# Eight convolution taps on TensorE in place of sixteen, an order for the early output products, and a wait ahead of GpSimd's additions

## The chip, the cores and the metric

The kernel runs on one core of one Trainium2 chip. The metric is the device time of one execution in microseconds (us). The profile is of one further execution; its span is the time from its first to its last instruction. Engines are named as in the profile: PE is TensorE's matmul, PEld its weight load, DVE is VectorE, ACT is ScalarE, POOL is GpSimd, SP is SyncE, which issues transfers.

## The reference

Two layers of an encoder block on 512 tokens of width 1024, in float32. Cut to what matters here:

```python
for l in range(2):
    x = x + 0.5 * swiglu(rms_norm(x, g1), w_gate1, w_up1, w_down1)     # 1024 -> 2816 -> 1024
    p = rms_norm(x, gm) @ w_in                                         # latents of q and k/v, 2 x 512 conv columns
    attn = mla_group(...)          # 8 heads of 96 (64 + 32 rotary), keys and queries RMS-normed, chunk-causal
    u = a * sigmoid(g)             # a, g: the conv columns of p, 512 each
    y = causal_depthwise_conv(u, conv_w) + conv_b                      # 31 taps, one filter per column
    conv = silu(layer_norm(y, lg, lb))
    x = x + concat([attn, conv], -1) @ w_out                           # 1024 -> 1024
    x = x + 0.5 * swiglu(rms_norm(x, g2), w_gate2, w_up2, w_down2)
    x = rms_norm(x, gp)
```

## The kernel before

`x` lies transposed in on-chip memory: 8 tiles of 128 features by 512 tokens. Each product of float32 operands is made of three matmuls (`mm3`, L165 to L169): both operands are split into a high and a low part (ScalarE casts the high part, VectorE subtracts for the low part: `split`, L171), and high x high, high x low and low x high are added up in one bank of PSUM. A `group` (L238) runs `mm3` over the tiles `k` of the contraction. Each layer is a feed-forward block (`ffn`), a mix block (`mix`) and another feed-forward block. The change lies wholly in `mix_body` (L629 to L1022), which is run once per layer.

The order of work within an engine is not that of the program text alone. A planner orders the instructions at build time by the text's order, by priorities (`tc.high_priority`) and by its own estimate of when each is ready, and on the chip every engine works its queue off in that fixed order. `tc.issue_after(i)` holds the instructions traced in its block behind `i` on the engine of `i`.

The mix block runs as follows.

- Projections: convolution columns, query latents, key latents. `keys` (L803) makes the keys of four token tiles. For each, GpSimd computes a reciprocal root (`rsqrt`, a power, L185), which is remembered as `order["keys"]` (L813), and VectorE scales the key tile `kn` (L815 to L819).
- The convolution's gated input `u` is in 4 chunks of 128 columns (`glu`, L640). `TAPS` says which engine makes the 31 taps of a chunk. Chunks 0 and 3 are summed by VectorE in a PSUM bank `acc` (L964). Chunks 1 and 2 are made in pairs: ScalarE multiplies `u` by one tap into a buffer `pr` (L968; four buffers), GpSimd adds it to `ys[c]` (L970). For chunk `PC` = 2 the first `PT` taps come from TensorE instead: `conv_pe` (L667), with 4 column groups of 32, against the diagonal matrices `diag` that GpSimd prepares (L632). The additions of chunk 1 from tap `PAUSE` = 16 on, and all of chunk 2, are held behind `order["keys"]` on GpSimd (L969). So are the transfers of the first four output weights `wo` (L949, L154), which GpSimd issues.
- Attention in eight heads, as a pipeline: transposes (L844, L849) and their eviction (L846, L851), `scores` (L868 to L876: matmul, maximum on VectorE, exponential on ScalarE), transposes of the probabilities (L891 to L894), `values` (L902 to L916), and the split of two heads' outputs into one of the four tiles of `at` (L173, L174). `conv_pe` stands between the steps of this pipeline.
- The convolution's layer norm is a chain at high priority (L986 to L997). GpSimd adds `ys[0]`, `ys[1]` and `ys[2]` (L988, L989), VectorE adds `ys[3]` (L990), TensorE makes the mean (`pm`, L992), VectorE subtracts it (L994), ScalarE squares and VectorE adds the squares (L203). TensorE sums them over the columns (`sums`, L210), VectorE, GpSimd and VectorE turn this into a scale per token (L217, L185, L225), and TensorE spreads it over the partitions (`spread`, L229). Then VectorE scales, ScalarE applies silu (L1006, L1008) and the results `cv` are split.
- The output product has 8 contraction tiles: 4 of `at`, 4 of `cv`. For the first `WOG` = 4 output tiles the `at` half is computed early, while the chain runs (`early_groups`, L978). Output tile 0 (`E1` = 1) stands in the text before the chain and tiles 1 to 3 behind it; all are held only behind the last head's scores on TensorE, and the planner fills them in. The `cv` half follows (L1012 to L1022).

Of the kernel before, what the change touches and what calls it, by code (L numbers as in the profile page):

```python
# [7 lines left out]
FP = mybir.dt.float32  # L8
# [4 lines left out]
ALU = mybir.AluOpType  # L13
AX = mybir.AxisListType

P = 128
D = 1024
S = 512
L = 2
KD = D // P  # L20
NT = S // P
H = 8
DN = 64
DR = 32
DQ = DN + DR
# [14 lines left out]
CHUNKS = ((0, 2), (2, 5), (5, 8), (8, 11))  # L40
TAPS = (0, 31, 31, 0)
Q = 32
PT = 16
PC = 2
PSTEP = 3
AHEAD = 2
# [4 lines left out]
GLUP = 0  # L51
EARLY = "s"
PRELOAD = 1
E1 = 1
WOG = 4
CHAIN = 400
WAKE = 10
# [6 lines left out]
VECS = [("g1", 8), ("gm", 8), ("g2", 8), ("gp", 8), ("gql", 3), ("gkl", 2),  # L64
        ("cw", 4 * CK), ("cb", 4), ("lg", 4), ("lb", 4), ("gq", 1), ("gk", 1), ("cp", PT)]
VOFF = {}
# [6 lines left out]
CI32 = 256  # L73
# [4 lines left out]
def encoder_kernel(ctx: ExitStack, tc: tile.TileContext, xT, consts, vecs, rgain, wgu1, wd1, wdq1,  # L78
# [11 lines left out]
    def nm(s):  # L90
        uid[0] += 1
        return f"{s}{uid[0]}"
# [4 lines left out]
    def tmp(w=S, dt=FP):  # L97
        return tmps.tile([P, w], dt, tag="t", name=nm("t"))

    def bank():  # L100
        return psum.tile([P, S], FP, tag="ps", name=nm("ps"))

    def behind(ins):
        stack = ExitStack()
        for i in ins:
            stack.enter_context(tc.issue_after(i))
        return stack

    def conv_bank():
        return psum.tile([P, S], FP, tag="cv", name=nm("cv"), bufs=1)  # L110

    def tiny(tag, w, dt=FP):
        return small.tile([P, w], dt, tag=tag, name=nm(tag))

    V, A, G, T = nc.vector, nc.scalar, nc.gpsimd, nc.tensor

    x = cpool.tile([P, KD, S], FP, name="x")
    cst = cpool.tile([P, CN], FP, name="cst")
# [12 lines left out]
    minus_half = cpool.tile([P, H], FP, name="minus_half")  # L131
# [10 lines left out]
    def vv(l, name):  # L142
        o, w = VOFF[name]
        return vec[:, l, o:o + w]

    def load_w(src, w, kind=""):
        raw = wpool.tile([P, WC], FP, tag="raw", name=nm("raw"), bufs=3)
        nc.sync.dma_start(out=raw[:, :w], in_=src)
        hi = wpool.tile([P, WC], FR, tag="wh", name=nm("wh"))
        order["cast"] = A.copy(hi[:, :w], raw[:, :w]).ins  # L150
        lo = low()
        if kind == "sum":
            A.activation(lo[:, :w], raw[:, :w], AF.Copy, scale=-1.0)
            G.dma_start(out=lo[:, :w], in_=src, accum_op=ALU.add)  # L154
            return hi, lo
        (G if kind in POOLW.split() else V).tensor_tensor(lo[:, :w], raw[:, :w], hi[:, :w].bitcast(FP),  # L156
                                                          ALU.subtract)
        return hi, lo
# [2 lines left out]
        return wpool.tile([P, WC], FR, tag="wl", name=nm("wl"))  # L161

    order = {}

    def mm3(o, lh, ll, rh, rl, first, last, free=False):  # L165
        T.matmul(o, lh, rh, start=first, stop=False, skip_group_check=free)  # L166
        T.matmul(o, lh, rl, start=False, stop=False, skip_group_check=free)  # L167
        order["mm"] = T.matmul(o, ll, rh, start=False, stop=last, skip_group_check=free).ins  # L168
        return order["mm"]  # L169
# [13 lines left out]
    def rsqrt(y, ve):  # L183

        return G.tensor_tensor(y, ve, minus_half[:, 0:y.shape[1]], ALU.pow).ins  # L185
# [36 lines left out]
    def spread(r, made=bank, dg=None):  # L222

        dg = tmp() if dg is None else dg
        V.tensor_tensor(dg.rearrange("p (t j) -> p t j", t=NT),  # L225
                        ident[:, None, :].to_broadcast([P, NT, P]),
                        r[:, :, None].to_broadcast([P, NT, P]), ALU.mult)
        ps = made()
        order["spread"] = T.matmul(ps, ones, dg, start=True, stop=True).ins  # L229
        return ps  # L230
# [7 lines left out]
    def group(o, w, rhs, ks, n, ts=slice(0, S)):  # L238

        for k in ks:  # L240
            c = slice(k * P, (k + 1) * P)
            order["product"] = mm3(o, w[0][:, c], w[1][:, c], rhs[k][0][:, ts], rhs[k][1][:, ts], k == 0, k == n - 1)
# [382 lines left out]
    def mix(l, gx, norm, done):  # L625
        with tc.tile_pool(name="k", bufs=4) as kpool:
            mix_body(kpool, l, gx, norm, done)

    def mix_body(kpool, l, gx, norm, done):  # L629
        u, order = [], {}  # L630
        diag = kpool.tile([P, PT, Q], FP, tag="m", name=nm("m"), bufs=11)
        G.tensor_tensor(diag, cst[:, None, CI32:CI32 + Q].to_broadcast([P, PT, Q]),  # L632
                        vv(l, "cp")[:, :, None].to_broadcast([P, PT, Q]), ALU.mult)
        shifted = []

# [31 lines left out]
        def conv_pe():  # L667

            ps = bank()
            for a in range(PT // 4):  # L670
                for i in range(4):
                    T.matmul(ps[i * Q:(i + 1) * Q, 4 * a:], diag[:, 4 * a + i], shifted[i][:, 0:S - 4 * a],  # L672
                             start=a == 0, stop=a == PT // 4 - 1)
            A.activation(ys[PC], ps, AF.Identity, bias=vv(l, "cb")[:, PC:PC + 1])
# [9 lines left out]
        kn = kpool.tile([P, NT, H, DQ], FP, tag="kn", name=nm("kn"), bufs=1)  # L684
# [109 lines left out]
        def up_kv(w, t, n=S):  # L794

            ts_ = slice(t * P, (t + 1) * P)
            ps = bank()
            for k in range(2):
                cs = slice(k * n, (k + 1) * n)
                mm3(ps, ckT[k][0][:, ts_], ckT[k][1][:, ts_], w[0][:, cs], w[1][:, cs], k == 0, k == 1)  # L800
            return ps

        def keys():  # L803
            wk = load_w(wkv[l, 0], WC, "uk")
            for t in range(NT):
                ps = up_kv(wk, t)
                A.copy(kn[:, t, :, 0:DN], ps.rearrange("p (h d) -> p h d", h=H))
                j = tmp()
                A.activation(j, ps, AF.Square)
                V.tensor_reduce(ssk[:, t], j.rearrange("p (h d) -> p h d", h=H), axis=AX.X, op=ALU.add)  # L810
                V.tensor_scalar(ssk[:, t], ssk[:, t], ckc[:, t:t + 1], None, ALU.add)
                sck = small.tile([P, H], FP, tag="sck", name=nm("sck"))
                order["keys"] = rsqrt(sck, ssk[:, t])  # L813
                scp = small.tile([P, H], FP, tag="scp", name=nm("scp"))
                V.tensor_scalar(scp, sck, ratio[:, t:t + 1], None, ALU.mult)  # L815
                V.tensor_tensor(kn[:, t, :, 0:DN], kn[:, t, :, 0:DN],
                                sck[:, :, None].to_broadcast([P, H, DN]), ALU.mult)
                V.tensor_tensor(kn[:, t, :, DN:DQ], cke[:, t, None, :].to_broadcast([P, H, DR]),  # L818
                                scp[:, :, None].to_broadcast([P, H, DR]), ALU.mult)  # L819


        first = groups([wcv[l, 0], wcv[l, 1]], gx)
# [12 lines left out]
        at = []  # L835
# [3 lines left out]
        heads = [{} for _ in range(H)]  # L839
# [109 lines left out]
        with tc.issue_after(order["keys"]):  # L949
            wo = [load_w(wout[l, m], WC, "sum") for m in range(WOP)]  # L950
        cw, cb = vv(l, "cw"), vv(l, "cb")
        for c, n in enumerate(TAPS):
# [4 lines left out]
            for s in range(n, CK):  # L957
                k = CK - 1 - s
# [6 lines left out]
            for s in range(PT if c == PC else 1, n):  # L965
                k = CK - 1 - s
# [8 lines left out]
                V.tensor_tensor(ys[c][:, n:], ys[c][:, n:], acc[:, n:], ALU.add)  # L975
        early = []

        def early_groups(ms):  # L978
            with tc.issue_after(heads[H - 1][EARLY]):
                for m in ms:  # L980
                    early.append(bank())
                    group(early[m], wo[m], at, range(4), KD)

        early_groups(range(E1))
        st = Stats()
        with tc.high_priority(CHAIN):  # L986
            ysum = u[1]
            G.tensor_tensor(ysum, ys[0], ys[1], ALU.add)  # L988
            G.tensor_tensor(ysum, ysum, ys[2], ALU.add)  # L989
            V.tensor_tensor(ysum, ysum, ys[3], ALU.add)  # L990
            pm = conv_bank()
            T.matmul(pm, onesm, ysum, start=True, stop=True)  # L992
            for c in range(4):
                V.tensor_tensor(ys[c], ys[c], pm, ALU.subtract)  # L994
                st.add(ys[c], eng=V, into=(u[2], u[1], diag.rearrange("p a b -> p (a b)"), u[1])[c])
            r = st.token(CW, conv_bank)
            pr = spread(r, conv_bank, u[1])  # L997
        if PRELOAD:
            with behind(heads[H - 1]["exps"]):
                A.activation(tiny("pre", 1), ysum[:, 0:1], AF.Silu)  # L1000
        early_groups(range(E1, WOG))
        lg, lb = vv(l, "lg"), vv(l, "lb")
        cv = []
        for c in range(4):
# [7 lines left out]
        for m0 in range(0, KD, WOG):  # L1012
            ms = range(m0, min(m0 + WOG, KD))
# [272 lines left out]
```

## Time and profile before

| | |
|---|---|
| Time, median of 3 runs | 1802.54 us (1801.73 to 1802.81) |
| The profiled execution's own time | 1799.38 us |
| Its span | 1797.6 us |
| PE, PEld busy | 1780.6 us (99%), 1579.2 us (88%) |
| DVE, ACT, POOL busy | 1501.2 us (84%), 1093.8 us (61%), 384.1 us (21%) |
| Granted TensorE clock | 0.999 |

Busy times are sums over the whole span; matmuls are pipelined, so that a full PE column is not PE at its peak. In layer 0 attention and convolution lie between about 437 and 522 us of the span, in layer 1 between about 1326 and 1411 us; a stretch of time says more there than the sums do. In a timeline a row has start, duration, engine, line and operation, output and inputs, count, and in brackets the engine's idle time before it and what ended it.

### The profile page before, as it was taken

The numbers are of one execution on the slowest core, as the hardware profiler recorded it, in microseconds if no ns is written. First come the engines' busy times: TensorE is split into PE (matmuls) and PEld (weight loads), VectorE is DVE, ScalarE is ACT, GpSimd is POOL, SyncE is SP. The second block draws the span as 40 slices with busy tenths as digits, with TensorE's granted clock in tenths as the row PEclk, the third lists the DMA queues.
The fourth block names the chain that finished last, engine by engine and source line by source line (L and its number), as shares of the span: only waits on it lengthen the run. The fifth ranks groups of instructions, "written<-read, shape, count | busy, mean of one in ns | idle before, by whom it ended". The sixth has DMA issues, their size and how long they took to land.

```text
span 1797.6 us, 29443 instructions
## 1 busy us (share of the span) xinstructions
PE 1780.6 (99%) x11430; PEld 1579.2 (88%) x11430; DVE 1501.2 (84%) x2309; ACT 1093.8 (61%) x1699; POOL 384.1 (21%) x313
## 2 busy tenths in 40 slices
PE   9999999999999999999999999999999999999998
PEld 7899999888668899999888999998976788999997
DVE  7898988589965989898779989876999568989883
ACT  5665756467853575756645666554777435657564
POOL 1000000258722000000310000002685310000002
PEclk9999999999999999999999999999999999999999
DMA  5657574325203466665426575743260136575742
GB/s 169 168 134 186 130 180 119 109 88 128 61 24 100 125 166 161 153 161 127 125 63 170 127 191 125 193 109 114 77 171 7 35 92 162 138 181 135 182 118 73
DMA packets 71947, 228.28 MB, mean 127 GB/s; under 512 B 8448, under 2 KB 9600, under 8 KB 71808
## 3 DMA queue, kind: packets, MB, share of 16 engines
q1 hardware_dynamic: 55536, 171.87, 30.6%
q0 software_dynamic: 16128, 54.53, 18.0%
q8 instruction: 89, 1.46, 0.3%
q14 instruction: 50, 0.41, 0.1%
q10 hardware_dynamic: 144, 0.00, 0.0%
HBM read 222.19 MB, written 2.10 MB: 125 GB/s over the span
## 4 chain that ended last, share of the span: by engine, by line
PE 89%; DVE 7%; ACT 1%; issue 1%; POOL 1%; DMA 1%; SPq 0%; ACTq 0%; DVEq 0%
PE ps L166 23%; PE ps L167 23%; PE ps L168 23%; PE ps L385 11%; PE ps L386 6%; DVE cv L964 1%; DVE mx L872 1%; PE ps L913 1%; POOL sck L185 1%; DVE r L894 0%; DVE kn L818 0%; PE ps L891 0%; PE ps L210 0%; DVE r L851 0%; PE ps L672 0%
## 5 line engine op out<-in xcount | busy, mean ns | idle before, releaser
L166 PE MATMUL ps<-r,wh 128*128 128x256 f32 (+1 forms) x2556 | 811.6, 321 | 6.8 <-ACT r L173 5.7
L167 PE MATMUL ps<-r,wh 128*128 128x256 f32 (+1 forms) x2556 | 813.5, 319 | 0.1
L168 PE MATMUL ps<-r,wl 128*128 128x256 f32 (+1 forms) x2364 | 755.6, 321 | 0.0
L166 PEld LDWEIGHTS ps<-r,wh 128*128 128x128 f32 x2556 | 483.7, 189 | 53.2 <-ACT r L173 7.3
L167 PEld LDWEIGHTS ps<-r,wh 128*128 128x128 f32 x2556 | 484.9, 190 | 36.7 <-DVE r L174 1.5
L168 PEld LDWEIGHTS ps<-r,wl 128*128 128x128 f32 x2364 | 448.6, 190 | 34.3 <-DVE wl L156 0.2
L385 PE MATMUL ps<-xj,wh 128*128 128x512 f32 x864 | 303.8, 391 | 0.0
L150 ACT CAST wh<-raw 128x1024 fp32r<-128x1024 f32 (+3 forms) x148 | 132.3, 900 | 210.1 <-PE ps L167 131.1
L256 ACT CAST wh<-fr 128x1024 fp32r<-128x1024 f32 (+1 forms) x160 | 157.8, 986 | 104.6 <-DVE fr L422 49.3
L402 POOL DMA_DIRECT2D ls<-in_wgu x72 | 62.5, 868 | 734.7 <-ACT ls L401 502.6
L156 DVE TENSOR_TENSOR wl<-raw,wh 128x1024 fp32r<-128x1024 f32 (+3 forms) x132 | 143.4, 1093 | 91.0 <-ACT wh L150 90.3
L258 DVE TENSOR_TENSOR wl<-fr,wh 128x1024 fp32r<-128x1024 f32 (+1 forms) x160 | 181.8, 1137 | 20.1 <-ACT wh L256 20.1
L385 PEld LDWEIGHTS ps<-xj,wh 128*128 128x128 f32 x864 | 161.4, 188 | 30.1
L386 PE MATMUL ps<-xj,ls 128*128 128x256 f32 x576 | 161.3, 280 | 0.0
L970 POOL TENSOR_TENSOR y<-y,pr 128x495 f32<-128x495 f32 (+29 forms) x90 | 121.7, 1353 | 46.4 <-ACT pr L968 41.0
L256 ACT CAST wh<-raw 128x1024 fp32r<-128x1024 f32 (+1 forms) x100 | 98.1, 981 | 45.1 <-PE ps L167 24.2
L258 DVE TENSOR_TENSOR wl<-raw,wh 128x1024 fp32r<-128x1024 f32 (+1 forms) x100 | 113.3, 1133 | 14.3 <-ACT wh L256 13.8
L386 PEld LDWEIGHTS ps<-xj,ls 128*128 128x128 f32 x576 | 108.3, 188 | 0.0
L401 ACT ACTIVATE ls<-fr 128x1024 fp32r<-128x1024 f32 (+1 forms) x56 | 56.1, 1002 | 75.6 <-PE ps L386 41.5
L203 POOL TENSOR_TENSOR r<-r,t 128x512 f32<-128x512 f32 x45 | 74.2, 1658 | 130.2 <-ACT t L199 129.7
L964 DVE SCALAR_TENSOR_TENSOR cv<-m,vec,cv 128x511 f32<-128x511 f32 (+14 forms) x120 | 87.8, 732 | 3.8 <-ACT cv L960 2.1
L402 POOL DMA_DIRECT2D ls<-in_wdq x32 | 27.6, 863 | 261.7 <-ACT ls L401 261.7
(257 smaller groups left out, 2925.1 us busy)
## 6 DMA issues: line engine op xcount, KB each, us to landing
fr<-in_wgu SPq DMA_DIRECT2D x112, 512.0 KB, 4.3
ls<-in_wgu POOLq DMA_DIRECT2D x72, 512.0 KB, 6.5
raw<-in_wgu SPq DMA_DIRECT2D x62, 512.0 KB, 4.6
fr<-in_wdq SPq DMA_DIRECT2D x48, 384.0 KB, 4.7
ls<-in_wdq POOLq DMA_DIRECT2D x32, 384.0 KB, 4.8
raw<-in_wd SPq DMA_DIRECT2D x32, 384.0 KB, 3.1
raw<-in_wd SPq DMA_DIRECT2D x32, 256.0 KB, 2.8
raw<-in_wcv SPq DMA_DIRECT2D x16, 512.0 KB, 3.5
```

Of the source, the lines that this page charges most:

```text
L150: order["cast"] = A.copy(hi[:, :w], raw[:, :w]).ins
L156: (G if kind in POOLW.split() else V).tensor_tensor(lo[:, :w], raw[:, :w], hi[:, :w].bitcast(FP), ALU.subtract)
L166: T.matmul(o, lh, rh, start=first, stop=False, skip_group_check=free)
L167: T.matmul(o, lh, rl, start=False, stop=False, skip_group_check=free)
L168: order["mm"] = T.matmul(o, ll, rh, start=False, stop=last, skip_group_check=free).ins
L256: A.copy(hi[:, :w], src[:, :w])
L258: order["lo"] = V.tensor_tensor(lo[:, :w], src[:, :w], hi[:, :w].bitcast(FP), ALU.subtract).ins
L385: T.matmul(o, w[0][:, c], both, start=start and k == 0, stop=False, skip_group_check=True)
L386: last = T.matmul(o[:, 0:HS], w[1][:, c], both[:, 0:HS], start=False, stop=k == 3, skip_group_check=True).ins
L402: G.dma_start(out=lo[:, :n], in_=w, accum_op=ALU.add)
L964: V.scalar_tensor_tensor(acc[:, s:], u[c][:, :S - s], tap(k), acc[:, s:], ALU.mult, ALU.add)
L970: order["conv"] = G.tensor_tensor(ys[c][:, s:], ys[c][:, s:], pr[:, s:], ALU.add).ins
```

## The change

`PT` goes from 16 to 8: TensorE makes 8 taps of chunk 2, and the 8 others become pairs of a ScalarE multiplication and a GpSimd addition (23 pairs for chunk 2 in place of 15). `order["keys"]` is no longer the last reciprocal root but a new one-element product on GpSimd that reads the last element of `kn` of the last token tile, which VectorE writes last. What was held behind `order["keys"]` is now held behind this product. The early products are cut into 16 steps of three matmuls each: contraction tiles 0 to 2 of the four output tiles, tile by tile, and then contraction tile 3 of all four. Steps 0 to 4 are held behind the last head's scores, steps 5 to 8 behind the `sums` matmuls of the layer norm, steps 9 to 15 behind its `spread`.

```diff
-PT = 16
+PT = 8
...
-E1 = 1
+EA = 5
+EB = 9
...
     order = {}
+
+    def ordered(name):
+        return order[name]
...
     def mix_body(kpool, l, gx, norm, done):
         u, order = [], {}
-        diag = kpool.tile([P, PT, Q], FP, tag="m", name=nm("m"), bufs=11)
-        G.tensor_tensor(diag, cst[:, None, CI32:CI32 + Q].to_broadcast([P, PT, Q]),
+        diag = kpool.tile([P, S // Q, Q], FP, tag="m", name=nm("m"), bufs=11)
+        G.tensor_tensor(diag[:, 0:PT], cst[:, None, CI32:CI32 + Q].to_broadcast([P, PT, Q]),
                         vv(l, "cp")[:, :, None].to_broadcast([P, PT, Q]), ALU.mult)
...
+            order["keys"] = G.tensor_tensor(tiny("kw", 1), kn[:, NT - 1, H - 1, DQ - 1:DQ], minus_half[:, 0:1],
+                                            ALU.mult).ins
...
-        def early_groups(ms):
-            with tc.issue_after(heads[H - 1][EARLY]):
-                for m in ms:
-                    early.append(bank())
-                    group(early[m], wo[m], at, range(4), KD)
-
-        early_groups(range(E1))
+        steps = [(m, k) for m in range(WOG) for k in range(3)] + [(m, 3) for m in range(WOG)]
+
+        def early_steps(a, b, behind_):
+            with tc.issue_after(behind_):
+                for m, k in steps[a:b]:
+                    if k == 0:
+                        early.append(bank())
+                    group(early[m], wo[m], at, (k,), KD)
+
+        early_steps(0, EA, heads[H - 1][EARLY])
...
             r = st.token(CW, conv_bank)
+            sums = ordered("sums")
             pr = spread(r, conv_bank, u[1])
+            spreading = ordered("spread")
...
-        early_groups(range(E1, WOG))
+        early_steps(EA, EB, sums)
+        early_steps(EB, len(steps), spreading)
```

## The prediction

> **What bounds the kernel now.** I read the page first, then busy time in stretches across one mix stage, then the timelines of single engines at the two ends of that stage.
>
> ```profile
> span 1797.6 us, 29443 instructions
> ...
> PE 1780.6 (99%) x11430; PEld 1579.2 (88%) x11430; DVE 1501.2 (84%) x2309; ACT 1093.8 (61%) x1699; POOL 384.1 (21%) x313
> ```
>
> TensorE is the bound over the span, so time is gained only where TensorE waits or is fed too slowly, and everything that the diff touches lies in the mix stage, which occurs twice. These are the stretches of layer 0 from the convolution on TensorE to the output product (columns: busy time and count of PE, PEld, DVE, ACT, POOL, then clock, DMA share, GB/s):
>
> ```profile
> 455.00:462.00 7.00, 7.00 (x62) 3.14 (x64) 6.44 (x12) 7.00 (x18) 6.61 (x6) 1.00 0.85 253
> 462.00:470.00 8.00, 8.00 (x65) 5.39 (x62) 8.00 (x17) 8.00 (x23) 7.68 (x8) 1.00 0.01 2
> 470.00:480.00 10.00, 9.96 (x88) 6.46 (x89) 9.93 (x20) 10.00 (x26) 9.45 (x8) 1.00 0.01 2
> 480.00:490.00 10.00, 9.66 (x82) 6.12 (x81) 10.00 (x21) 6.71 (x20) 4.54 (x4) 1.00 0.01 2
> 490.00:502.00 12.00, 12.00 (x109) 8.13 (x106) 11.22 (x23) 6.41 (x17) 0.00 (x0) 1.00 0.00 1
> 502.00:512.00 10.00, 10.00 (x47) 6.75 (x45) 5.59 (x9) 3.43 (x6) 0.00 (x0) 1.00 0.01 2
> 512.00:522.00 10.00, 7.16 (x34) 5.36 (x33) 4.01 (x7) 4.23 (x7) 1.03 (x1) 1.00 0.00 0
> ```
>
> Here the limit changes. To 480 us VectorE and ScalarE are both full; to 502 us VectorE is nearly full, ScalarE half idle and GpSimd empty; in the last row TensorE is busy 7.16 of 10 us, so 2.84 us are lost. The same stretch of layer 1 has the same hole:
>
> ```profile
> 1401.00:1411.00 10.00, 7.16 (x34) 5.36 (x33) 3.73 (x7) 3.95 (x6) 1.03 (x1) 1.00 0.00 0
> ```
>
> **Part 1: the ordered early products.** TensorE's timeline at the end of the stage: mean (L992), sums of squares (L210), spread of the scale (L229), first product of a convolution row (L166).
>
> ```profile
> 500.58 1.12 PE L992 MATMUL cv<-m,onesm 128*128 128x512 f32 x2
> ...
> 503.42 0.39 PE L168 MATMUL ps<-m,wl 128*128 128x512 f32 x1
> 503.65 0.40 PE L166 MATMUL ps<-r,wh 128*128 128x512 f32 x1
> ...
> 512.18 0.95 PE L210 MATMUL cv<-ones,m 128*128 128x1 f32 x8
> ...
> 517.48 1.02 PE L229 MATMUL cv<-m,ones 128*128 128x512 f32 x2
> 521.34 1.20 PE L166 MATMUL ps<-r,wh 128*128 128x512 f32 x4 [2.84 <-ACT r L173]
> ```
>
> And the two VectorE rows that feed L210 and L229:
>
> ```profile
> 504.14 2.27 DVE L203 TENSOR_TENSOR m<-m,m 128x512 f32<-128x512 f32 x3
> ...
> 514.47 0.69 DVE L225 TENSOR_TENSOR m<-cst,rtok 128x512 f32<-128x512 f32 x1 [1.14 <-POOL rtok L185]
> ```
>
> The squares are summed at 504.14 + 2.27 = 506.41, but TensorE reaches the sums at 512.18: the wait is its own queue of early products. The scale is ready at 514.47 + 0.69 = 515.16 and its spread starts at 517.48, again behind early products. After the spread no early product is left, and TensorE idles 2.84 us while VectorE, ScalarE make the first operand. An early matmul takes 503.65 - 503.42 = 0.23 us. There are 48 (4 groups x 4 steps x 3). From 512.18 to 517.48, less the sums' 0.95, is room for about 19; so about 29 stood before the sums and none after the spread.
>
> The change fixes 5 steps (15 matmuls) ahead of the sums, 4 steps (12) between sums and spread, 7 steps (21) behind the spread. With everything earlier unmoved: sums are reached 14 x 0.23 = 3.2 us earlier, at about 509.0, still 2.6 us behind their input. The scale needs 515.16 - 512.18 = 2.98 us from the sums' start, so it is there at 512.0; TensorE has done sums and 12 matmuls (0.95 + 2.76) at 512.7, 0.7 us later. From the spread's start to the first convolution product passed 521.34 - 517.48 = 3.86 us, so that operand is ready at 516.6; TensorE has done the spread and 21 matmuls (1.02 + 4.83) at 518.55, 1.9 us later. Every wait is covered, the narrowest by 0.7 us. The gain is the hole, 2.84 us a layer; next late is TensorE itself. The four steps that need the last heads' output are the last in the list, so they cannot hold up the sums. Bounds: 2.84 to nothing (if the scale chain came over 2 us later relative to TensorE, the cover would be gone). I take 2.84, since both covers come from rows.
>
> **Part 2: GpSimd's additions wait for the keys.** VectorE at the keys, with GpSimd adding beside it, then the same two operations over all their occurrences (min/median/max in ns), and the wait of TensorE:
>
> ```profile
> 437.56 2.34 DVE L818 TENSOR_TENSOR kn<-cke,scp 128x256 f32<-128x256 f32 x1
> 439.83 1.94 DVE L815 TENSOR_SCALAR scp<-sck,ratio 128x8 f32<-128x8 f32 x1
> 441.69 0.68 DVE L816 TENSOR_TENSOR kn<-kn,sck 128x512 f32<-128x512 f32 x1
> 442.29 1.46 DVE L818 TENSOR_TENSOR kn<-cke,scp 128x256 f32<-128x256 f32 x1
> ```
> ```profile
> L818 DVE TENSOR_TENSOR kn<-cke,scp x8: 415/940/2352, 435.5 to 1330.9; 128x256 f32<-128x256 f32 x8
> ```
> ```profile
> L815 DVE TENSOR_SCALAR scp<-sck,ratio x8: 215/228/1946, 432.7 to 1328.5; 128x8 f32<-128x8 f32 x8
> ```
> ```profile
> 443.80 0.31 PE L849 MATMUL ps<-cst,kn 128*96 128x128 f32 x1 [0.88 <-DVE kn L818]
> ```
>
> At their shortest the four would take 0.42 + 0.22 + 0.68 + 0.42 = 1.74 us; they took 442.29 + 1.46 - 437.56 = 6.19. The new one-element product waits for the last key, so the additions behind it cannot start before, and 4.45 us of VectorE are freed. TensorE had other matmuls to do until 0.88 us before 443.80, so most of that was hidden. What is sure is at most 0.88 us; the upper end is 4.45, if VectorE could use all of it ahead of its full stretch; the lower end zero, if what follows waits for something else. I take 0.6 a layer, near TensorE's own wait, because VectorE's queue has a fixed order and its next entries need TensorE's results.
>
> On why it is slow, the Trainium skill (SBUF — State Buffer, Who interferes with whom) says that VectorE operations with two SBUF inputs and GpSimd operations that read SBUF lock each other out of a shared port for a whole instruction; the 2.34 us beside 0.42 agree. By that rule a VectorE operation with one input in PSUM would not be slowed by more additions.
>
> What is queued behind the new wait on GpSimd: the four output-weight transfers and 38 additions. Its timeline:
>
> ```profile
> 437.41 0.91 POOL L154 DMA_DIRECT2D wl<-in_wout  x1
> ...
> 464.45 18.66 POOL L970 TENSOR_TENSOR y<-y,pr 128x495 f32<-128x495 f32 x14
> 483.18 1.60 POOL L989 TENSOR_TENSOR m<-m,y 128x512 f32<-128x512 f32 x1
> ```
>
> **Part 3: 8 taps moved from TensorE.** TensorE does 16 instead of 32 of these a layer, and the score behind them is what VectorE waited for:
>
> ```profile
> 455.92 3.60 PE L672 MATMUL ps<-r,m 128*32 128x512 f32 x32
> ```
> ```profile
> 460.22 0.42 DVE L872 TENSOR_REDUCE mx<-ps 128x1 f32<-128x256 f32 x1 [0.46 <-PE ps L870]
> ```
>
> That frees 1.8 us of TensorE, but from 462 on VectorE and ScalarE are full, so only VectorE's idle time in 455 to 462 (7.00 - 6.44 = 0.56) can be won: 0 to 0.56; I take 0.4, near the 0.46 that it waited. The Trainium skill (Perfetto Trace Analysis, Identifying the Most-Contended Engine) says that matmul busy time misjudges TensorE and that weight-load busy time is the measure; that is 3.14 of 7.00 us here, so by the rule TensorE has room and the 16 matmuls earn nothing (0.8 us less in the sum). The 0.46 wait says a little more.
>
> GpSimd gets 8 additions a layer: 18.66 / 14 = 1.33 us each, 10.7 us. It ended its sum (L989) at 484.78. Its start moves from 437.41 to the end of the keys, 437.56 + 1.74 = 439.3, and the new product comes on top: nearest is the 1.14 us that VectorE waited for a small GpSimd operation (the row of L225), nothing at best; I take 0.3, since it has one element. That is 2.2 us. So L989 ends at 484.78 + 10.7 + 2.2 = 497.7, less what the additions themselves win where VectorE no longer locks them; against this is what VectorE needs:
>
> ```profile
> 498.01 0.64 DVE L990 TENSOR_TENSOR m<-m,m 128x512 f32<-128x512 f32 x1
> ```
>
> It is in time by 0.3 us, and behind L990 (done 498.65) the mean on TensorE starts only at 500.58, another 1.9 us. So I cost the additions at nothing; the cover is the 2.2 us, and each us beyond costs one us of TensorE.
>
> ScalarE gets 8 multiplications, by this row 0.69 us each, 5.5 us a layer:
>
> ```profile
> 478.15 1.37 ACT L968 ACTIVATE pr<-m,vec 128x483 f32<-128x483 f32 x2
> ```
>
> GpSimd's four buffers pace them, so they fall after 479.5, one per 1.33 us, to about 490. There ScalarE has 10 - 6.71 = 3.3 us idle and, to 502, another 5.6. At most 5.5 - 3.3 = 2.2 us do not fit and push exponentials back; at best none. I take 0.7, since the softmax steps of several heads overlap.
>
> Last, VectorE splits that now meet GpSimd:
>
> ```profile
> L174 DVE TENSOR_TENSOR r<-y,r x4: 682/687/692, 523.3 to 1413.1; 128x512 fp32r<-128x512 f32 x4
> L174 DVE TENSOR_TENSOR m<-t,m x2: 1644/1645/1646, 482.0 to 1371.3; 128x512 fp32r<-128x512 f32 x2
> ```
>
> The second form ran inside GpSimd's additions: 0.96 us more. With additions until 497 one further split a layer can meet them: 0 to 0.96, taken as 0.3. The halved preparation of the tap matrix on GpSimd lies far ahead of any of this and costs nothing either way.
>
> **Sum.** A layer: -2.84 - 0.6 - 0.4 + 0.7 + 0.3 = -2.84; two layers -5.7. The profiled execution took 1799.38 us (span 1797.6 and 1.78 around it), so 1793.7 for such a run; the median of the runs is 1802.54, 3.16 above, so the forecast is 1796.8. The bounds without a rival: best -2.84 - 0.88 - 0.56, twice, -8.6 (1794.0); worst -2.84 + 2.2 + 0.96, twice, +0.6 (1803.2).
>
> **Rivals.**
> 1. GpSimd becomes the bound (slower). L989, beside VectorE's work, took 1.60 us for one addition. If all 38 additions took that: 60.8 us, and with four transfers and two sums (4 x 0.91 + 2 x 1.60 = 6.8) they end at 439.6 + 67.6 = 507.2. L990 then ends at 507.8, and the mean comes 7.3 us after its 500.58; less 2.84, +4.4 a layer: 1811.4. It decides from 1.48 us an addition ((500.58 + 2.84 - 0.64 - 439.6 - 6.8) / 38). Against it: 1.33 measured over 14. Chance 0.14.
> 2. ScalarE returns the gain: multiplications ahead of exponentials in a queue that is already full to 480 us; the worst bound above, 1803.2. For it: ScalarE and VectorE are both at 100% from 462 to 480, so a shift of either counts. It also stands for a planner that places the sums or steps so that the hole stays. Chance 0.18.
> 3. VectorE does use the freed time: all limits up to 502 us are VectorE's, and 4.45 us at the keys come out of its queue. If about 3 are kept: -2.84 - 3 - 0.4 a layer, -12.5: 1790.1. Against it: its next entries need TensorE, which is busy to 443 us. Chance 0.16.
>
> **How the numbers follow.** The forecast has 0.52. About 0.2% (3.6 us) is what a measurement of this kernel can tell from no change. Forecast and rival 3 are faster by more: 0.68; rival 2 is the same: 0.18; rival 1 slower: 0.14. The range goes from 1789, just under rival 3, to 1803.5, just over rival 2; it leaves out rival 1 and little below.
>
> **What would show it.** TensorE's 2.84 us wait before the first L166 of the convolution rows is gone in both layers; sums come about 3 us after their input or sooner and the spread soon after its own; 21 early matmuls stand behind the spread. L818 and L815 take 0.4 and 0.2 us throughout; L672 shows 16 a layer. L989 ends at 495 to 498 us and L990 does not wait for it. The forecast is wrong if VectorE waits for GpSimd at L990, if ScalarE waits for GpSimd's buffers ahead of exponentials by some us a layer, or if TensorE idles ahead of the sums because 15 matmuls are too few to cover the squares.

## The result, and the profile after

The changed kernel takes 1794.47 us (median of 7 runs, 1794.07 to 1800.19), the kernel before 1802.54 us; the ratio is 0.9966, with a 95% interval of 0.9956 to 0.9976. The profiled execution took 1794.1 us, that of before 1799.38. The forecast was 1796.8 us in a range of 1789.0 to 1803.5, and faster.

The head of the page of after:

```profile
span 1792.3 us, 29423 instructions
...
PE 1777.1 (99%) x11398; PEld 1580.9 (88%) x11398; DVE 1487.8 (83%) x2309; ACT 1101.1 (61%) x1715; POOL 404.4 (23%) x331
```

The stretches of layer 0 that the prediction showed, in after (same columns):

```profile
455.00:462.00 7.00, 6.50 (x54) 3.12 (x51) 6.68 (x14) 7.00 (x20) 6.53 (x7) 1.00 0.93 267
462.00:470.00 8.00, 7.13 (x54) 4.53 (x54) 8.00 (x17) 8.00 (x22) 7.76 (x7) 1.00 0.06 25
470.00:480.00 10.00, 9.51 (x90) 7.01 (x90) 9.93 (x20) 10.00 (x26) 9.37 (x9) 1.00 0.00 0
480.00:490.00 10.00, 9.23 (x81) 6.17 (x79) 10.00 (x21) 10.00 (x25) 9.45 (x8) 1.00 0.01 2
490.00:502.00 12.00, 12.00 (x102) 7.76 (x100) 10.76 (x22) 9.51 (x24) 8.78 (x7) 1.00 0.01 2
502.00:512.00 10.00, 10.00 (x62) 7.06 (x59) 6.39 (x12) 3.40 (x6) 1.03 (x1) 1.00 0.00 0
512.00:522.00 10.00, 10.00 (x44) 7.89 (x43) 5.75 (x9) 6.50 (x10) 0.00 (x0) 1.00 0.01 2
```

The last row, 7.16 before, is full: the hole is gone. Between 455 and 490 us TensorE now idles 0.50 + 0.87 + 0.49 + 0.77 = 2.63 us, where it idled 0.38 before, and ScalarE is full to 490 us (10.00 where it had 6.71).

The timeline of TensorE at the end of the stage in after. Lines have moved: mean L1001, sums L214, spread L233, `mm3` L170 to L172.

```profile
500.80 1.02 PE L1001 MATMUL cv<-m,onesm 128*128 128x512 f32 x2
...
503.63 0.50 PE L170 MATMUL ps<-m,wh 128*128 128x512 f32 x1
...
509.70 0.95 PE L214 MATMUL cv<-ones,m 128*128 128x1 f32 x8
...
513.37 1.02 PE L233 MATMUL cv<-m,ones 128*128 128x512 f32 x2
...
518.81 0.39 PE L172 MATMUL ps<-r,wl 128*128 128x512 f32 x1
519.04 1.07 PE L170 MATMUL ps<-r,wh 128*128 128x512 f32 x4
```

Between the first early product and the sums lie 15 early matmuls, 12 stand between sums and spread, 21 behind the spread, and the first product of the convolution rows follows without a wait (no bracket), where before it had 2.84 us.

It helps to cut the span at GpSimd's reciprocal roots (`rtok`), one of which stands at the head of every normalization. "Mix" is from the root ahead of the mix stage to the one behind it:

| us | to mix 0 | mix 0 | feed-forward | feed-forward | mix 1 | to the end | span |
|---|---|---|---|---|---|---|---|
| before | 360.26 | 206.21 | 340.15 | 342.96 | 208.01 | 340.01 | 1797.6 |
| after | 361.68 | 202.33 | 340.89 | 344.21 | 202.36 | 340.83 | 1792.3 |
| difference | +1.42 | -3.88 | +0.74 | +1.25 | -5.65 | +0.82 | -5.3 |

So the mix stages won 9.5 us, and 4.2 us were lost where the change touches nothing. The 1.42 us at the start include one wait for a weight that is still on its way (1.2 us, below). The loss outside shows in one group of the feed-forward blocks' matmuls, first before, then after (us of all, mean ns of one):

```profile
L385 PE MATMUL ps<-xj,wh 128*128 128x512 f32 x864 | 303.8, 391 | 0.0
```
```profile
L389 PE MATMUL ps<-xj,wh 128*128 128x512 f32 x864 | 306.5, 393 | 0.0
```

The same 864 matmuls take 2.7 us more. The 576 of the next line (L386, then L390), which read the same tile `xj`, go from 161.3 to 162.3 us. This and the gain in the mix stages are what the experiments take apart.

No time or wait below is read from the profile of wait_only: that execution took 1932.6 us at a mean granted clock of 0.848.

### The profile page after: what moved, and what is told of

It reads as the page before. It is cut to its first block, busy times and chain, and to the rows that moved or that the text cites. A ratio compares the mean times of both kernels' runs of the same rounds, so it can differ in the third digit from the quotient of the medians.

```text
span 1792.3 us, 29423 instructions
## 1 busy us (share of the span) xinstructions
PE 1777.1 (99%) x11398; PEld 1580.9 (88%) x11398; DVE 1487.8 (83%) x2309; ACT 1101.1 (61%) x1715; POOL 404.4 (23%) x331
## 4 chain that ended last, share of the span: by engine, by line
PE 92%; DVE 4%; ACT 1%; issue 1%; DMA 1%; POOL 0%; SPq 0%; ACTq 0%; DVEq 0%
PE ps L170 24%; PE ps L171 23%; PE ps L172 23%; PE ps L389 11%; PE ps L390 6%; DVE cv L970 1%; PE ps L919 1%; DVE mx L878 1%; PE ps L874 1%; PE ps L897 1%; PE ps L214 0%; DVE wl L262 0%; DMA r<-m 0%; PE ps L912 0%; DVE r L900 0%
## 5 line engine op out<-in xcount | busy, mean ns | idle before, releaser
L170 PE MATMUL ps<-r,wh 128*128 128x256 f32 (+1 forms) x2556 | 810.4, 320 | 2.7 <-ACT wh L1114 1.2
L172 PE MATMUL ps<-r,wl 128*128 128x256 f32 (+1 forms) x2364 | 755.3, 321 | 0.0
L170 PEld LDWEIGHTS ps<-r,wh 128*128 128x128 f32 x2556 | 485.2, 190 | 48.0 <-ACT wh L151 3.7
L172 PEld LDWEIGHTS ps<-r,wl 128*128 128x128 f32 x2364 | 449.1, 190 | 34.1 <-DVE wl L157 0.4
L389 PE MATMUL ps<-xj,wh 128*128 128x512 f32 x864 | 306.5, 393 | 0.0
L389 PEld LDWEIGHTS ps<-xj,wh 128*128 128x128 f32 x864 | 161.5, 188 | 31.1
L390 PE MATMUL ps<-xj,ls 128*128 128x256 f32 x576 | 162.3, 282 | 0.0
L976 POOL TENSOR_TENSOR y<-y,pr 128x503 f32<-128x503 f32 (+29 forms) x106 | 141.2, 1333 | 47.5 <-ACT pr L974 40.6
L390 PEld LDWEIGHTS ps<-xj,ls 128*128 128x128 f32 x576 | 108.8, 189 | 0.0
```

Of the source, the lines that this page charges most:

```text
L389: T.matmul(o, w[0][:, c], both, start=start and k == 0, stop=False, skip_group_check=True)
L390: last = T.matmul(o[:, 0:HS], w[1][:, c], both[:, 0:HS], start=False, stop=k == 3, skip_group_check=True).ins
L976: order["conv"] = G.tensor_tensor(ys[c][:, s:], ys[c][:, s:], pr[:, s:], ALU.add).ins
```

## The experiments

Each was timed in five rounds in turn with the kernel before, whose median in the three groups was 1801.11 (order_only to order_wait), 1801.59 (order_pad to all_shared, steps_ahead) and 1801.04 us (the rest). The last column is the group of 864 matmuls above; its line is L388 to L390, as the edits move it.

| kernel | median (range), us | ratio to before (95%) | mix 0, mix 1 in the profile | L389's group |
|---|---|---|---|---|
| order_only | 1792.09 (1791.61 to 1793.28) | 0.9949 (0.9937 to 0.9962) | 203.03, 203.03 | 303.8 |
| taps_only | 1800.22 (1799.12 to 1802.55) | 0.9995 (0.9986 to 1.0003) | 208.79, 206.08 | 303.9 |
| wait_only | 1803.03 (1801.48 to 1805.32, and the one of 1932.6) | 1.0010 (1.0001 to 1.0019) | not used | not used |
| order_wait | 1794.07 (1793.62 to 1794.64) | 0.9960 (0.9947 to 0.9974) | 202.36, 202.41 | 306.5 |
| order_pad | 1795.75 (1794.91 to 1797.49) | 0.9968 (0.9956 to 0.9981) | 203.02, 203.00 | 306.5 |
| order_wait_shared | 1790.29 (1789.37 to 1791.34) | 0.9938 (0.9925 to 0.9950) | 202.18, 202.14 | 303.8 |
| all_shared | 1790.62 (1790.35 to 1794.71) | 0.9944 (0.9931 to 0.9958) | 202.78, 202.32 | 303.9 |
| wait_shared | 1797.94 (1795.39 to 1802.77) | 0.9990 (0.9981 to 0.9999) | 206.93, 205.53 | 303.9 |
| steps_ahead | 1802.74 (1800.60 to 1804.30) | 1.0004 (0.9996 to 1.0013) | 207.78, 206.24 | 306.5 |
| two_behind | 1797.37 (1794.77 to 1799.62) | 0.9979 (0.9970 to 0.9988) | 204.76, 204.76 | 303.9 |
| taps4_shared | 1807.77 (1806.34 to 1808.80) | 1.0038 (1.0025 to 1.0051) | 210.38, 209.99 | 303.9 |

### The parts alone

**order_only**: after, with the taps and the wait undone.

```diff
-PT = 8
+PT = 16
...
-            order["keys"] = G.tensor_tensor(tiny("kw", 1), kn[:, NT - 1, H - 1, DQ - 1:DQ], minus_half[:, 0:1],
-                                            ALU.mult).ins
```

> Only the ordered early products; 16 taps on TensorE and the old place of the wait. Theory A (the gain is TensorE's idle time ahead of the first convolution product, 2.84 us in each layer): the wait before that product is gone in both layers and the time falls by about 5.7 us, ratio near 0.9968. Theory B (the gain is TensorE's work on the taps): no change, within 1 us. Theory C (the gain is VectorE's time at the keys): no change, within 1 us.

It is faster than the whole change. Its TensorE timeline has no wait before the convolution rows, but still the wait for the keys:

```profile
444.17 0.32 PE L853 MATMUL ps<-cst,kn 128*96 128x128 f32 x1 [0.89 <-DVE kn L822]
...
509.31 0.95 PE L214 MATMUL cv<-ones,m 128*128 128x1 f32 x8
...
512.99 1.02 PE L233 MATMUL cv<-m,ones 128*128 128x512 f32 x2
...
518.64 1.07 PE L170 MATMUL ps<-r,wh 128*128 128x512 f32 x4
```

The mix of layer 0 goes from 206.21 to 203.03, -3.18 us, of which 2.84 are the hole. The order accounts for the gain, and the other two parts together have cost something: 2.4 us by the medians.

**taps_only**: before, with 8 taps on TensorE.

```diff
-PT = 16
+PT = 8
```

> Only 8 in place of 16 taps on TensorE; old early products, old wait. Theory A: the hole of 2.8 us stays, and the moved taps by themselves make between -0.8 and +6 us in all (the bounds of the terms of the prediction), most likely +1; ratio near 1.0005. Theory B: 1.8 us of TensorE in each layer, -3.6 us, ratio near 0.998. Theory C: no change.

Nothing to measure: the interval holds 1. With the order and the wait in place the taps move nothing either (order_wait to after: 1794.07 to 1794.47 us, mix 202.36 to 202.33).

**wait_only**: before, with the one-element product alone.

```diff
+            order["keys"] = G.tensor_tensor(tiny("kw", 1), kn[:, NT - 1, H - 1, DQ - 1:DQ], minus_half[:, 0:1],
+                                            ALU.mult).ins
```

> Only the wait of GpSimd's additions for the keys; 16 taps, old early products. Theory A: -0.6 us in each layer, -1.2 in all, since TensorE has other work while VectorE is slow; L818 at 0.4 us. Theory C: VectorE keeps most of the 4.45 us it gets back, 3 us or more in each layer, -6 us in all, ratio near 0.9967. Theory B: no change.

It is no gain, and if anything a loss of 0.1%.

**order_wait**: after, with the taps undone.

```diff
-PT = 8
+PT = 16
```

> Ordered early products and the wait for the keys, with 16 taps on TensorE: the change without its taps. Theory A: -5.7 - 1.2 = -6.9 us, ratio near 0.9962, as fast as the whole change or slightly faster, since the 8 additional pairs of multiplication and addition are not there. Theory B: 3 us or more slower than the whole change.

The mix stages gain about 0.65 us each over order_only (203.03 to 202.36 and 202.41), yet the kernel is 2 us slower. So the wait does what it should, and something outside of the mix stage costs more. In order_wait the L389 group takes 306.5 us, in order_only 303.8.

### The wait or the place of its tile

The new tile `kw` has one column of its own in on-chip memory, so whatever is laid out behind it can move (no run recorded where a tile lies). Two theories: the place costs (S), or the wait does (W).

**order_pad**: order_only, with a column of that name that is written once at the start and never read. No wait.

```diff
+    V.memset(tiny("kw", 1), 1.0)
```

> order_only, and at the start one more tile of one column in the pool of small tiles (as large as the tile that the new one-element product writes), filled once and never read; no wait. order_only took 1792.09 us and its feed-forward matmuls L389 303.8 us, while the whole change and order_wait have 306.5 us there and lose 2.8 us in the feed-forward blocks. Theory S (the new tile moves all later tiles in on-chip memory, and the joined feed-forward matmuls are slower at that place): L389 at 306.5 us and 1794.9 us. Theory W (the wait itself, by the order it gives to the rest): L389 stays at 303.8 and the time at 1792.1.

**order_wait_shared**: order_wait, with the product written into a small buffer that is there already. The wait stays, and no tile is added.

```diff
-            order["keys"] = G.tensor_tensor(tiny("kw", 1), kn[:, NT - 1, H - 1, DQ - 1:DQ], minus_half[:, 0:1],
+            order["keys"] = G.tensor_tensor(tiny("gqs", 1), kn[:, NT - 1, H - 1, DQ - 1:DQ], minus_half[:, 0:1],
```

> order_wait with the one-element product written into the two buffers that the scaled query gain uses, so that no tile is added. Theory S: L389 back at 303.8 us; the mix stages stay as short as in order_wait (202.4 us from the reciprocal root before to the one behind, 0.65 less than order_only), so 1794.07 - 2.7 = 1791.3 us. Theory W: 1794.1.

The group of joined matmuls in order_pad, then in order_wait_shared:

```profile
L390 PE MATMUL ps<-xj,wh 128*128 128x512 f32 x864 | 306.5, 393 | 0.0
```
```profile
L389 PE MATMUL ps<-xj,wh 128*128 128x512 f32 x864 | 303.8, 391 | 0.0
```

The added column costs, not the wait: a column that nobody reads makes order_only 3.7 us slower and lengthens the group by 2.7 us; the wait without a column of its own is at 1790.29 and 303.8. Every profile with the column has 306.5 us in this group, every one without it 303.8 or 303.9. That the column costs by moving other tiles is the reading that is left, not a measurement; why these matmuls should care where their tiles lie, no run shows.

**all_shared** (after, with the same edit) and **wait_shared** (before, with the wait alone, in the shared buffer) put the same question to the whole change and to the wait.

> The whole change with the one-element product in the same two buffers. Theory S: 1794.47 - 2.7 = 1791.8 us, L389 at 303.8. Theory W: 1794.5. Theory A (the taps earn nothing beside the order and the wait): within 1 us of order_wait_shared.

> The kernel before with the wait for the keys alone, its product in the shared buffers, so that no tile moves. wait_only took 1803.03 us, 1.9 more than before, with an added tile that by order_pad costs about 2.8 to 3.7. Theory S and the 0.65 us a layer seen between order_only and order_wait: 1801.3 - 1.3 = 1800.0 us. Rival (without the order the wait only moves the early end of the keys into the hole ahead of the convolution products): 1801.3.

Sharing takes 3.9 us off the whole change (1794.47 to 1790.62) and turns the wait alone from a loss (1.0010) into a small gain (0.9990, 1.8 us, where 1.3 was expected). all_shared and order_wait_shared are within 0.4 us of each other and are the fastest kernels of this study: with the buffer shared, the order and the wait are the whole gain. Whether TensorE makes 8 taps or 16 makes 0.3 us by the medians, and 8 are no faster.

### The order

**steps_ahead**: after, with 12 steps ahead of the sums, 4 between, none behind the spread.

```diff
-EA = 5
-EB = 9
+EA = 12
+EB = 16
```

> The whole change with 12 early steps ahead of the sums, 4 between sums and spread and none behind the spread (EA = 12, EB = 16). Theory A: TensorE idles again about 2.8 us ahead of the first convolution product in each layer, and the time goes back up by 5.7 us to about 1800.2. Rival (the order gains by something else, the place of the sums in the queue not mattering): no hole, within 1 us of the whole change.

The hole is back, to a hundredth of a microsecond, and the whole gain is lost. TensorE's timeline in steps_ahead:

```profile
513.77 0.95 PE L214 MATMUL cv<-ones,m 128*128 128x1 f32 x8
...
518.79 1.02 PE L233 MATMUL cv<-m,ones 128*128 128x512 f32 x2
...
522.65 1.61 PE L170 MATMUL ps<-r,wh 128*128 128x512 f32 x4 [2.84 <-ACT r L177]
```

That is theory A (the order closes the hole) against the taps and the keys, which are both still in this kernel. But the loss is 8.3 us by the medians (6.8 by the ratios to before) against the 5.7 of two holes. The stretches of before behind its hole in layer 0 and in layer 1, and those of steps_ahead behind its hole in layer 0, show what comes on top (the column behind POOL is the granted clock):

```profile
520.00:525.00 5.00, 3.66 (x16) 3.05 (x17) 3.45 (x6) 4.27 (x8) 0.00 (x0) 1.00 0.01 2
...
1410.00:1415.00 5.00, 4.38 (x12) 3.48 (x13) 2.88 (x5) 3.54 (x7) 0.00 (x0) 0.66 0.00 0
```
```profile
520.00:525.00 5.00, 2.35 (x7) 1.87 (x8) 3.46 (x6) 4.43 (x8) 0.00 (x0) 0.82 0.00 0
525.00:530.00 5.00, 5.00 (x20) 4.04 (x19) 1.46 (x3) 0.57 (x2) 0.00 (x0) 0.84 0.00 0
```

Behind one of its two holes the granted clock falls, here to 0.66 over 5 us, which is 0.34 x 5 = 1.7 us of TensorE. In finer slices it stands at a half, and at a half 1.7 us are lost in about 3.4 (before, layer 1):

```profile
1406.00:1411.00 5.00, 2.16 (x8) 1.10 (x8) 2.88 (x5) 2.50 (x5) 0.00 (x0) 1.00 0.00 0
1411.00:1414.00 3.00, 3.00 (x9) 2.33 (x8) 1.76 (x4) 2.54 (x5) 0.00 (x0) 0.50 0.00 0
```

It falls behind one of the two holes in each of the four profiles read here that have two of 2.84 us: before in layer 1 (mix 208.01 against 206.21), taps_only, wait_shared and steps_ahead in layer 0 (208.79 against 206.08, 206.93 against 205.53, 207.78 against 206.24). After and order_only, without the hole, show 1.00 in these stretches of both layers. Why only one of two holes does it, no run shows. The Trainium skill (TensorE: Matmul & The Clock Gate, What's actually happening) says that the array is cut to half its clock behind an idle window of about 3.4 us and gets it back after as long a busy one. The half and the 3.4 us agree with the trace of before; the idle time does not, since these waits of 2.84 us are shorter than that window and the clock falls behind one in two.

**two_behind**: all_shared, with 8 steps ahead, 6 between and two behind the spread, to make a shorter hole.

```diff
-EA = 5
-EB = 9
+EA = 8
+EB = 14
```

> all_shared with 8 early steps ahead of the sums, 6 between and 2 behind the spread (EA = 8, EB = 14): 6 matmuls, 1.4 us, cover the end of the chain. Theory H (TensorE waits 2.84 - 1.38 = 1.46 us in each layer, too short to take the granted clock down): 1790.6 + 2.9 = 1793.5 us, and clock 1.00 in every 5 us behind the wait. Rival (the clock falls behind any wait): as with no step behind the spread a further 2 us or so in one of the layers, 1795.5, and a stretch with a clock below 0.9.

```profile
519.90 1.19 PE L170 MATMUL ps<-r,wh 128*128 128x512 f32 x4 [1.47 <-ACT r L177]
```

In the profile the hole of 1.47 us costs 2.0 to 2.4 us a layer against all_shared, at a clock of 1.00 behind it. The timed runs say more: 1797.37 is 6.8 us above all_shared, not the 3 of two such holes, so that both expectations (1793.5 and 1795.5) were too low, and the runs spread over 5 us. The mean granted clock of each execution is on record. It is 0.997 or 0.998 in five of the eleven (1797.37 to 1799.62 us) and 1.000 in four (1795.69 to 1796.93 us); 1.7 us of lost clock are 0.001 of it. Without a hole it is 0.997 in only 3 of 32 executions (order_only, order_wait, order_pad, order_wait_shared, all_shared and after). So the clock does seem to fall in some executions with a wait of 1.47 us, which theory H had ruled out; no trace shows where. Even at 1.000 the kernel is 5 us or more above all_shared, and what exceeds the holes stays open.

### The limit of GpSimd

**taps4_shared**: all_shared, with four taps on TensorE: four more additions a layer.

```diff
-PT = 8
+PT = 4
```

> all_shared with 4 taps on TensorE instead of 8, so 4 more pairs of multiplication and addition a layer. In the whole change GpSimd's last sum ends at 499.26 us and VectorE waits 0.24 us for it: its cover is used up. Theory G (from here GpSimd is the bound, and each us beyond the cover costs a us): 4 x 1.33 = 5.3 us a layer later, less TensorE's saving of at most 0.9, so +4.4 a layer and 1790.6 + 8.8 = 1799.4 us; VectorE waits about 5 us for GpSimd at its last addition. Rival (the early products behind the spread cover a late chain): +2.5 a layer or less, 1795 at most.

It costs 17.2 us, twice what was expected. GpSimd's last sum, VectorE's addition behind it, and TensorE's mean and sums, from the timelines of the three engines:

```profile
501.99 1.84 POOL L998 TENSOR_TENSOR m<-m,y 128x512 f32<-128x512 f32 x1
```
```profile
503.87 0.69 DVE L999 TENSOR_TENSOR m<-m,m 128x512 f32<-128x512 f32 x1 [1.18 <-POOL m L998]
```
```profile
507.74 1.02 PE L1001 MATMUL cv<-m,onesm 128*128 128x512 f32 x2
...
514.13 1.86 PE L214 MATMUL cv<-ones,m 128*128 128x1 f32 x8 [4.45 <-DVE m L207]
...
516.86 0.63 PE L172 MATMUL ps<-r,wl 128*128 128x512 f32 x1
517.29 0.63 PE L170 MATMUL ps<-m,wh 128*128 128x512 f32 x1
...
519.95 0.39 PE L171 MATMUL ps<-r,wh 128*128 128x512 f32 x1
520.18 0.39 PE L172 MATMUL ps<-r,wl 128*128 128x512 f32 x1
```

GpSimd ends at 503.83, and VectorE waits 1.18 us for it, not the 5 that were expected; its addition is done at 504.56. But the mean starts only at 507.74. In after it starts at 500.80, ahead of all early matmuls; here the planner's order has attention's last work and 11 early matmuls ahead of it. Only four of the 15 early matmuls ahead of the sums are left to cover VectorE's subtractions and squares, and TensorE idles 4.45 us. Behind this wait the matmuls follow each other every 0.43 us (517.29 - 516.86) in place of 0.23, until about 519.5, and the granted clock has fallen again:

```profile
515.00:520.00 5.00, 5.00 (x16) 4.14 (x17) 0.85 (x2) 1.49 (x2) 1.04 (x1) 0.54 0.00 0
```

It falls in both layers here (0.62 from 1410 to 1415 us). So GpSimd's later end, which is the condition of rival 1, is dearer than the prediction had it, for two reasons: the mean moved back in TensorE's queue, and the clock fell. Four taps with the mean held at its old place were not tried, so what GpSimd alone would cost is not known.

## Why the prediction was right, and where it was not

**The main mechanism was right; the sum came out by luck.** Against its own basis, the profiled execution, -5.7 us was forecast and -5.3 came. But -9.5 came from the mix stages and +4.2 from elsewhere, and neither figure was forecast. That the two errors nearly cancel is luck. The 3.8 us beyond the forecast in the mix stages are, over both layers, 1.7 of clock, 0.8 more from the order, 0.1 more from the keys (order_wait), and 1.3 because the terms of the taps were not paid.

By medians it is -8.1, since the profiled execution of before was 3.16 us below its median and that of after 0.4. The forecast of 1796.8 carried the 3.16 over as if it were the same for both kernels. The granted clocks fit another reading: in the three groups 18 of 57 executions of before have a mean of 0.999, as the profiled one has (median 1799.7 us), and the other 39 a lower one (median 1801.7), while the clock of after is 0.999 or more in five of seven.

**Part 1, the order: right in mechanism, too small.** Everything before the mix stage ends 1.42 us later in after, so 1.42 is taken off its times. The sums then start at 508.28 (forecast 509.0) and the spread at 511.95 (512.7), the 21 matmuls stand behind it, and TensorE reaches the convolution rows at 517.62 (518.55). These times hold the gain at the keys too; order_only, which has the order alone and comes to its mix stage 0.35 us later than before, has 508.96, 512.64 and 518.29 on the scale of before, all within 0.3 us of the forecast. Every cover held. From VectorE's timeline in after, the input of sums and that of the spread:

```profile
507.54 0.68 DVE L207 TENSOR_TENSOR m<-m,m 128x512 f32<-128x512 f32 x1
...
511.99 0.69 DVE L229 TENSOR_TENSOR m<-cst,rtok 128x512 f32<-128x512 f32 x1 [1.15 <-POOL rtok L189]
```

The sums come 1.5 us after their input (508.22), the spread 0.7 us after its own. The term was -2.84 a layer; it measured -3.2 (order_only, layer 0), of which 0.3 is not explained, and in layer 1 -5.0, of which 1.7 are the clock behind the hole. That clock was not in the sum at all. The row that tells it lay just past the stretch that the prediction quoted (1401 to 1411 us); the next 5 us have 0.66.

**Part 2, the keys: right.** -0.6 was forecast. Against order_only, about -0.65 came in order_wait, and -0.85 and -0.89 in order_wait_shared, which has no tile more than order_only: the whole of TensorE's wait. VectorE's and GpSimd's timelines in after:

```profile
438.98 0.41 DVE L822 TENSOR_TENSOR kn<-cke,scp 128x256 f32<-128x256 f32 x1
439.32 0.22 DVE L819 TENSOR_SCALAR scp<-sck,ratio 128x8 f32<-128x8 f32 x1
...
443.63 0.69 DVE L646 TENSOR_TENSOR t<-ps,r 128x512 f32<-128x512 f32 x1 [3.17 <-PE ps L172]
```
```profile
440.55 0.19 POOL L824 TENSOR_TENSOR kw<-kn,minus_half 128x1 f32<-128x1 f32 x1 [1.67 <-DVE kn L822]
```

The operations take 0.41 and 0.22 us, and then VectorE waits 3.17 us for TensorE: the freed time could not be used, as the prediction argued against rival 3, which falls. Only TensorE's wait of 0.89 was to be had. The new product took 0.19 us (forecast 0.3). What it costs besides is the column for its output, which no step had.

**Part 3, the taps: the cover as forecast, the three small terms not.** GpSimd's last sum and VectorE's addition behind it in after:

```profile
497.65 1.61 POOL L998 TENSOR_TENSOR m<-m,y 128x512 f32<-128x512 f32 x1
```
```profile
499.29 0.69 DVE L999 TENSOR_TENSOR m<-m,m 128x512 f32<-128x512 f32 x1 [0.24 <-POOL m L998]
```

It ends at 499.26, on before's scale 497.84; 497.7 was forecast. VectorE waits 0.24 us for it, where "does not wait" was forecast; this was one of the signs that the prediction had named against itself. It costs nothing: VectorE's addition is done at 499.98 and the mean starts at 500.80, so 0.8 of the 2.2 us of cover are left. Four more additions (taps4_shared) went past it. The terms -0.4, +0.7 and +0.3 add up to +0.6 a layer; measured is none from order_wait to after (202.36 to 202.33 in layer 0), and +0.6 and +0.2 from order_wait_shared to all_shared. The term for the splits can be read alone: the split that took 1.64 us before takes 0.68 in order_wait and in after, and one other in after takes 1.04 in place of 0.68. How the other two share was not measured singly, but the waits of TensorE in after (us in total, times, longest) show two effects that cancel:

```profile
PE ps L874 <- ACT r L882: 1.7, 4, 0.5
PE ps L850 <- ACT r L882: 1.4, 4, 0.4
PE ps L170 <- ACT wh L1114: 1.2, 1, 1.2
...
PE ps L912 <- ACT r L882: 1.0, 2, 0.5
```

The 8 moved taps free 16 matmuls of 0.11 us, 1.8 us a layer, and TensorE spends the time waiting, for the most part for exponentials of the full ScalarE: in the four stretches from 455 to 490 us it is busy 34.79 of 35 us in order_wait and 32.37 in after. Rival 2's mechanism is real, but it gave back only what the taps had freed, and the order's gain stayed. ScalarE itself waits for no buffer of GpSimd between 437 and 502 us, which was another sign against the forecast. The rule of the Trainium skill (Perfetto Trace Analysis, Identifying the Most-Contended Engine) that the prediction set beside this, that matmul busy time misjudges TensorE, agrees in that the taps earned nothing (taps_only 0.9995). The third row is the wait at the start of the span.

**Not in any step: the added column.** The prediction costed the new product at its own time on GpSimd (0.3 us) and its output at nothing. The output made +2.8 us in the last three feed-forward stretches of the profile, and 3.7 to 3.9 us in the timings (order_only to order_pad, after to all_shared).

**Rival 1** did not come (22 additions in 29.67 us are 1.35 each, 1.48 decides), and taps4_shared shows that four more additions are enough to open a wait.

## What to carry to other kernels

Where the bounding engine waits at the end of a chain and has independent work, count that work, count each link of the chain, and fix how many pieces stand ahead of each link; a wait closed in this way can be worth more than its length, since the clock may fall behind it. Work taken off the bounding engine earns nothing while another engine paces it: look at who is full in that stretch, not at the busy share of the span. When a part that does its work in the profile makes the kernel slower, compare groups that the change does not touch, and try the same edit without a new buffer.

## What the runs showed of the hardware that was not expected

- Behind a wait of 2.84 us of TensorE the granted clock fell to 0.57 to 0.84 over 5 us stretches (taps_only below), behind one of the two such waits of an execution, in four profiles of four. The loss was 1.7 us in before, wait_shared and steps_ahead, and twice that in taps_only (0.43 x 5 + 0.26 x 5 = 3.45). Behind a wait of 4.45 us it was as long as in taps_only, in both layers (taps4_shared). Behind 1.47 us it did not fall in the one profile, but five of the eleven timed executions had a lower mean clock.

```profile
520.00:525.00 5.00, 3.63 (x9) 2.90 (x10) 3.46 (x6) 4.28 (x8) 0.00 (x0) 0.57 0.00 0
525.00:530.00 5.00, 5.00 (x18) 4.01 (x17) 0.17 (x1) 0.00 (x0) 0.00 (x0) 0.74 0.00 0
```

- One column more in on-chip memory, never read, lengthened 864 matmuls of another stage from a mean of 391 to 393 ns, and the kernel by 3.7 us (order_only to order_pad).
